# A macaron decoder block on one core: twelve up products of the second tile as three rounded passes, and the first seven-product tile with its low parts last

## The chip, the cores and the metric

The kernel runs on one core of one Trainium2 chip. TensorE (PE) multiplies 128x128 weight blocks with activations into PSUM; VectorE (DVE), ScalarE (ACT) and GpSimd (POOL) do the elementwise work; SP issues most of the loads from HBM, ACT and POOL a few. All transfers run on the core's 16 DMA engines; in the profile q1 is the queue that SP's issues use, q0 the one of POOL's. A transfer issued from POOL can add what it brings to what lies in SBUF already (an accumulating transfer). The metric is the device time of one execution in microseconds (us), lower is better.

## The reference, cut to what matters

```python
h = h + 0.5 * _swiglu(_rms_norm(h, ffn1_norm), ffn1_w_gate, ffn1_w_up, ffn1_w_down)
m, p, c, s = _hybrid_mixer(_rms_norm(h, mix_norm), ...)
h = h + m
h = h + 0.5 * _swiglu(_rms_norm(h, ffn2_norm), ffn2_w_gate, ffn2_w_up, ffn2_w_down)
y = _rms_norm(h, final_norm)
# _swiglu(x, wg, wu, wd) = (silu(x @ wg) * (x @ wu)) @ wd
```

520 tokens (512 of a prompt, 8 single ones), 1024 features, 2816 hidden features, all in float32. The change lies in the first feed-forward block, the first 45 us of the program.

## The kernel before, in words

Tokens are the columns of a product: two halves of 260. Features lie on the partitions, in eight groups of 128, which are also taken as four pairs: group j of the first depth half with group j of the second. A hidden tile is 128 hidden features; the block has 22 of them, named by f. Each needs a gate product and an up product over the 1024 features (u = 0 and 1); the weight of one is a 128x1024 float32 tile of 512 KB, `raw`, loaded by SP. There is room for two pairs of raws, so tile 2 takes the place of tile 0 and tile 3 that of tile 1, and each load waits until the readers of what lies there are done.

The opening handles tiles 0 and 1 with plain float32 products (`plain`): for each of gate and up there are 4 pairs x 2 depth halves x 2 token halves = 16 products of 128x260. On TensorE one plain product shows as two weight loads and two matmuls. The results are called P_00 (tile 0's gate), P_01 (its up), P_100 and P_101 (the two token halves of tile 1's gate) and P_11 (tile 1's up). P_11 comes last of the opening.

From tile 2 on the kernel splits each operand into a rounded part (hi) and the rest (lo) and multiplies hi by hi, hi by lo and lo by hi, in three passes of one record each (`mm3`, lines 147, 150 and 151). It also uses a scheme of seven products in place of eight over the 2x2 blocks of depth and tokens; the products are numbered 1 to 7 and run on tile 2 in the order 1, 2, 5, 6, 3, 7, then the first of tile 3, then 4. For it the weights are added up first: s1 (read as `c`) and s2 (read as `d`) are sums of quarters of the gate and up weights, so one tile needs the parts of four things: whi_a and wlo_a (the first raw), shi_c and slo_c, shi_d and slo_d, qhi_b and qlo_b (a quarter). Products 1 and 2 read a, 5 and 7 read c, 6 and 3 read d, 4 reads b.

The parts of a weight are made in one of two ways. `part` and `split` (line 135 and 137) cast hi on ScalarE and subtract on VectorE. `part_by_dma` (lines 242 to 244) casts hi on ScalarE, copies its negative into lo on ScalarE, and lets POOL add the weight from HBM to it by an accumulating transfer. For tile 2, s1 itself is made by transfers: SP brings two quarters and POOL adds a third (line 421).

The activations have been prepared in the same opening. Of each pair the four blocks of depth and token half lie in `xg`, slots 0 to 3; the rounded parts of slots 0, 1 and 2 (and of three sums, the rest of the seven) lie in xth (hi) and xtl (lo). Slot 3, the first depth half with the second token half, has no rounded part of its own.

A scheduler sets the order on each engine from the code, with priorities and a few fixed places (`tc.high_priority`, `queued`, `keep_in_program_order`); each engine then runs its own list in order, and an instruction that waits holds up all behind it on that engine. Around the change ScalarE runs the last casts of xth, a table load and two square roots for the norm (line 209), copies of P_00 to P_101, then the cast whi_2a, shi_2c, qhi_2b, another table load and the silu of tiles 0 and 1 (line 364). VectorE makes wlo_2a, the first half of s2 (line 425), slo_2c, the gate product of tile 0 (line 366), the second half of s2 (line 426), the gate product of tile 1 and slo_2d (both subtractions on line 137).

Of the kernel before, what the change touches and what calls it, by code (L numbers as in the profile page):

```python
# [10 lines left out]
F32 = mybir.dt.float32  # L11
F32R = mybir.dt.float32r
AF = mybir.ActivationFunctionType
ALU = mybir.AluOpType
# [3 lines left out]
P = 128  # L18
# [4 lines left out]
HB = NT // 2  # L23
HALVES = (slice(0, HB), slice(HB, NT))
KD = D // P
# [9 lines left out]
CHUNKS = (8, 8, 6)  # L35
LOW_ON_DVE = ((2, 0), (3, 0), (KF - 1, 1))
ON_ACT = 4
STATES = ((1, 1, 1, 1), (6, 17, 19, 20, 21), 4)
OUT_LOW_BY_DMA = ((1, 0), (1, 1))
LOW_BY_DMA = {1: (2, 3, 4, 5, 6), 2: (*range(7), 9, 11)}  # L40
# [24 lines left out]
def tile_trunk_step(ctx: ExitStack, tc: tile.TileContext, ins: dict, outs: dict):  # L65
    nc = tc.nc
# [9 lines left out]
    ps = [None]  # L76
# [43 lines left out]
    def weight_homes(n, name, hp, nb, tags):  # L120
        if hp is wp:
            popped = len(homes) > 1
            hp, nb, tags = homes.pop(0) if popped else homes[0]
            if third and not popped:
                third.append(name)
                if len(third) % 3 == 0:
                    return tuple(t[:, :n] for t in third[0])
        return tuple(hp.tile([P, 1024], F32R, tag=t, bufs=nb, name=f"{t}_{name}")[:, :n] for t in tags)

    def split(src, n, name, hp, nb, tags, then=()):  # L130
        hi, lo = weight_homes(n, name, hp, nb, tags)
        h, l = hi, lo
        if len(src.shape) == 3:
            h, l = (t.rearrange("p (j c) -> p j c", j=src.shape[1]) for t in (hi, lo))
        cast = nc.scalar.copy(h, src)  # L135
        with queued(*then):
            low = nc.vector.tensor_tensor(out=l, in0=src, in1=h.bitcast(F32), op=ALU.subtract)
        ends[:] = cast.ins, low.ins
        return hi, lo
# [23 lines left out]
    def ws(w, k, m=P):  # L163
        return w[:, k * m : (k + 1) * m]
# [76 lines left out]
    def part_by_dma(hi, lo, s, home):  # L241
        nc.scalar.copy(hi, s)
        nc.scalar.activation(out=lo, in_=hi.bitcast(F32), func=AF.Copy, scale=-1.0)
        nc.gpsimd.dma_start(out=lo, in_=home, accum_op=ALU.add)
# [22 lines left out]
    class Ffn:  # L267
# [26 lines left out]
        def plain(self, f, xg, j, us=(0, 1), pin=False):  # L294
            for u in us:
# [8 lines left out]
                for q in range(2):  # L304
                    for b, slot in enumerate(((0, 1), (3, 2))):
# [3 lines left out]
                        if pin and q == b == 0:  # L309
                            tc.keep_in_program_order(mm)  # L310

        def keep(self, f, us):

            for u in us:
                t = self.plain_kept[f, u] = self.gate_home(f) if u == 0 else self.wx.tile(
                    [P, 2, HB], F32, tag="ac", bufs=3, name=f"ac{self.i}_{f}")
                bs = self.banks[f, u]
                if len(bs) == 3:
                    copied = nc.scalar.copy(t, bs[2][:, :, :HB])
                else:  # L320
                    for b in range(2):
                        copied = nc.scalar.copy(t[:, b], bs[b][:, :HB])
            return copied.ins
# [77 lines left out]
        def sums(self, f, n, src, raw, d1, by_dma):  # L401
            i, wx = self.i, self.wx
            s1 = wx.tile([P, 2, 512], F32, tag="sw", bufs=3 - i, name=f"s1_{n}")
            s2 = wx.tile([P, 2, 512], F32, tag="sw", bufs=2, name=f"s2_{n}") if i == 1 else None
            if i == 2 and isinstance(f, int) and f < 4:
                s2 = self.qs[1].rearrange("p (q c) -> p q c", q=2)
            if isinstance(f, int):
                halves = [raw[:, u].rearrange("p (q c) -> p q c", q=2) for u in range(2)]
                up0 = halves[1][:, 0].unsqueeze(1).to_broadcast([P, 2, 512])
                diag = bass.AP(up0.tensor, up0.offset - 1024, [up0.ap[0], (1536, 2), up0.ap[2]])  # L410
            else:
                halves = [raw[:, u].rearrange("p (j q c) -> p q j c", q=2, c=P) for u in range(2)]
                up0 = halves[1][:, 0].unsqueeze(1).to_broadcast([P, 2, 4, P])
                diag = bass.AP(up0.tensor, up0.offset - 1024, [up0.ap[0], (1024 + P, 2), *up0.ap[2:]])
                s1, s2 = (t if t is None else t.rearrange("p q (j c) -> p q j c", j=4) for t in (s1, s2))
            if by_dma:
                low = src[2 * f + 1][:, :512].unsqueeze(1).to_broadcast([P, 2, 512])
                queue = nc.sync if i == 1 else nc.gpsimd
                queue.dma_start(out=s1[:, 0], in_=src[2 * f][:, :512])
                queue.dma_start(out=s1[:, 1], in_=src[2 * f + 1][:, 512:])  # L420
                nc.gpsimd.dma_start(out=s1, in_=low, accum_op=ALU.add)
            else:
                nc.vector.tensor_tensor(out=s1, in0=diag, in1=up0, op=ALU.add)  # L423
            s2 = halves[0] if s2 is None else s2
            nc.vector.tensor_tensor(out=s2[:, 0], in0=s1[:, 1], in1=halves[0][:, 0], op=ALU.add)
            nc.vector.tensor_tensor(out=s2[:, 1], in0=s2[:, 0], in1=halves[0][:, 1], op=ALU.add)
            flat = "p q c -> p (q c)" if isinstance(f, int) else "p q j c -> p (q j c)"
            s1 = s1.rearrange(flat)
            if len(s2.shape) == 3 or i == 1:
                s2 = s2.rearrange(flat)  # L430
            with tc.high_priority() if by_dma else nullcontext():
                e1 = split(s1, 1024, f"{n}c", wx, 2, ("shi", "slo"))
            e2 = split(s2, 1024, f"{n}d", wx, 2, ("shi", "slo"))
            if f == 2:
                self.behind[3] = tuple(ends), (), False
            first, second = (range(4), range(4, 8)) if isinstance(f, int) else (range(0, 8, 2), range(1, 8, 2))
            self.w[f] = {1: (d1, first), 2: (d1, second), 7: (e1, range(4)), 5: (e1, range(4, 8)), 6: (e2, range(4)),
                         3: (e2, range(4, 8))}
            self.held[f] = halves[1][:, 1]
            if i == 1:  # L440
                self.quarter(f)
# [17 lines left out]
        def product(self, f, p):  # L459
            js = range(KD // 2)  # L460
            if f not in self.A:
                self.load(f, *self.behind.get(f, ((), (), False)))
                n = f"{self.i}_{f}"
                self.A[f] = ps[0].tile([P, 512], F32, tag="A", bufs=2, name=f"A{n}")
                self.BE[f] = ps[0].tile([P, 2, 512], F32, tag="BE", bufs=2, name=f"BE{n}")
                self.ac[f] = [self.wx.tile([P, 2, HB], F32, tag="ac", bufs=3, name=f"ac{n}_{q}") for q in range(2)]
            if p != 1 and 4 not in self.w[f]:
                self.quarter(f)
            slot, dst, opens = {1: (0, 0, True), 2: (1, 1, True), 5: (3, 2, True), 6: (5, 0, False),
                                3: (2, 2, False), 7: (4, 0, False), 4: (6, 0, False)}[p]  # L470
            opens = opens and (p != 2 or f in self.whole)
            out = self.A[f] if dst == 0 else self.BE[f][:, dst - 1]
            (whi, wlo), k = self.w[f][p]
            xth, xtl = self.nx[:2]
            if isinstance(f, int):
                xs = [[x[:, j, slot] for j in js] for x in (xth, xtl)]
            else:
                u = {5: 6, 6: 5}.get(slot, slot)
                xs = [[self.gs[f.c * CHUNKS[0] // 2 + j][:, q, u] for j in js] for q in range(2)]
            wh, wl = ([ws(w, k[j]) for j in js] for w in (whi, wlo))  # L480
            pin = self.i == 1 or f != 1
            if self.i == 2:
                mm_low_last(out[:, :HB], wh, wl, *xs, opens, pin, skip_group_check=True)
            else:
                for j in js:
                    mm3(out[:, :HB], wh[j], wl[j], xs[0][j], xs[1][j], opens and j == 0, j == js[-1],
                        pin=pin and j == 0, skip_group_check=True)
            a, c = self.ac[f]
            if p == 1 and f not in self.whole:
                a = self.BE[f][:, :, :HB]  # L490
            keep = {1: a[:, 0], 6: a[:, 1], 7: c[:, 0], 5: c[:, 1]}.get(p)
            if keep is not None:
                self.copied = nc.scalar.copy(keep, out[:, :HB]).ins  # L493
                if (f, p) == (2, 7):
                    self.tail = self.copied
            if p == 7:
                nc.vector.tensor_tensor(out=c[:, 0], in0=c[:, 0], in1=c[:, 1], op=ALU.add)
# [226 lines left out]
    with tc.high_priority():  # L724
# [3 lines left out]
            late.pop(0)()  # L728
        with queued(root, recip):
            late.pop()()  # L730
    for j in range(KD // 2):
        ffn1.plain(1, xg1[j], j, (1,))
    with tc.high_priority(), queued(root):
        ffn1.keep(1, (0,))
    with tc.high_priority():
# [717 lines left out]
```

## Time and profile before

| what | value |
|---|---|
| median of 3 runs | 958.22 us (957.04 to 959.76) |
| the profiled execution | 956.44 us, span 954.7 us |
| granted TensorE clock in it | 0.996 |
| TensorE busy | 942.1 us, 7652 matmul records |
| VectorE / ScalarE busy | 854.0 us / 635.7 us |
| bytes read from HBM | 129.72 MB |

The span is the time between the first and the last instruction that the profiler saw. A row of instructions in order of time has its start, its length, the engine, the line, the operation and what it writes and reads; a bracket tells how long the engine sat idle before it and what ended that. Matmuls overlap, so their pace is read from start to start. A row of waits tells who waited for whom, the total in us, how often and the longest. A row of transfers ends with KB each and the median us from issue to landing; a row of a queue has packets, MB and the share of the 16 engines.

### The profile page before, as it was taken

The page shows a single profiled execution, that of the slowest core. Times are in us where ns is not written, and L with a number is a line of the kernel's source. Part 1 is how long each engine was busy: PE and PEld are TensorE (multiplying, and loading weights), DVE is VectorE, ACT ScalarE, POOL GpSimd, SP SyncE. Part 2 cuts the span into 40 slices and gives each one's busy share as a digit, 9 for nine tenths or more (in the row PEclk, how much of TensorE's full clock was granted, in tenths as well). Part 3 has the DMA queues.
Part 4 walks back from the last instruction along what each step waited for, and adds up shares of the span by engine and source line. Part 5 has one row for each costly group of instructions (what it writes and reads, how often), then busy time and mean ns, then how long its engine had stood idle before and what let it go on. Part 6 is the DMA issues. An engine that isn't in the chain of part 4 may idle for free. (4 is left out here: it accounts for less than half of the span.)

```text
span 954.7 us, 19636 instructions
## 1 busy us (share of the span) xinstructions
PE 942.1 (99%) x7652; PEld 925.0 (97%) x7652; DVE 854.0 (89%) x1462; ACT 635.7 (67%) x1178; POOL 148.9 (16%) x230
## 2 busy tenths in 40 slices
PE   9999999999999999999999999999999999999996
PEld 8999999999999999999999999999999999999995
DVE  6899899998988688789989998999989899899886
ACT  7777756677566465474768745777776766776763
POOL 0011100101000001046352000112122111122120
PEclk9999999999999999999999999999999999999998
DMA  7666554555553243353265444457667656767642
GB/s 213 179 164 154 141 157 125 122 137 151 141 147 101 81 139 116 90 185 133 97 179 163 119 121 122 112 122 179 170 165 183 158 124 158 183 166 188 171 147 90
DMA packets 53917, 138.34 MB, mean 145 GB/s; under 512 B 7672, under 2 KB 15800, under 8 KB 53824
## 3 DMA queue, kind: packets, MB, share of 16 engines
q1 hardware_dynamic: 39840, 104.18, 34.5%
q0 software_dynamic: 13712, 32.78, 18.5%
q8 instruction: 60, 0.98, 0.4%
q14 instruction: 33, 0.27, 0.1%
q10 hardware_dynamic: 272, 0.13, 0.0%
HBM read 129.72 MB, written 7.34 MB: 144 GB/s over the span
## 5 line engine op out<-in xcount | busy, mean ns | idle before, releaser
L493 ACT COPY ac<-A 128x260 f32<-128x260 f32 x85 | 31.7, 373 | 37.2 <-PE A L161 18.5
L423 DVE TENSOR_TENSOR s<-raw 128x1024 f32<-128x1024 f32 x39 | 47.5, 1218 | 2.7 <-DMA raw<-in_w1gu 1.4
L493 ACT COPY ac<-BE 128x260 f32<-128x260 f32 x41 | 15.4, 377 | 35.2 <-PE BE L161 16.9
L147 PE MATMUL inx<-xh_mx,whi_inx 128*128 128x260 f32 x112 | 31.8, 284 | 0.0
L150 PE MATMUL inx<-xl_mx,whi_inx 128*128 128x260 f32 x112 | 31.6, 282 | 0.0
L151 PE MATMUL inx<-xh_mx,wlo_inx 128*128 128x260 f32 x112 | 31.6, 282 | 0.0
L994 DVE SCALAR_TENSOR_TENSOR A<-U,h,A 128x544 f32<-128x544 f32 x36 | 28.9, 802 | 1.6 <-ACT A L992 1.2
L306 PE MATMUL P<-x,raw 128*128 128x260 f32 x128 | 28.9, 386 | 0.0
L306 PEld LDWEIGHTS P<-x,raw 128*128 128x128 f32 x128 | 24.5, 193 | 4.1 <-DMA raw<-in_w1gu 0.4
L1160 ACT ACTIVATE so<-br,sxdt 128x128 f32<-128x128 f32 x64 | 22.7, 376 | 7.7 <-DVE room L1162 6.9
L156 PE MATMUL wo<-catg,whi_wo 128*128 128x260 f32 x192 | 27.4, 285 | 0.0
L156 PEld LDWEIGHTS wo<-catg,whi_wo 128*128 128x128 f32 x192 | 24.8, 188 | 0.2
L135 ACT CAST thi<-raw 128x1024 fp32r<-128x1024 f32 (+1 forms) x14 | 14.2, 1013 | 15.3 <-PE wo L156 4.8
L1271 DVE TENSOR_TENSOR h<-wo,h 128x260 f32<-128x260 f32 x48 | 19.2, 422 | 5.0 <-PE wo L161 4.8
L248 DVE TENSOR_TENSOR gs<-gq,gs 128x780 fp32r<-128x780 f32 (+1 forms) x28 | 23.1, 826 | 0.0
L147 PE MATMUL inz<-xh_mx,whi_inz 128*128 128x260 f32 x80 | 22.9, 287 | 0.0
L150 PE MATMUL inz<-xl_mx,whi_inz 128*128 128x260 f32 x80 | 22.7, 284 | 0.0
L151 PE MATMUL inz<-xh_mx,wlo_inz 128*128 128x260 f32 x80 | 22.6, 283 | 0.0
L147 PEld LDWEIGHTS inx<-xh_mx,whi_inx 128*128 128x128 f32 x112 | 21.1, 188 | 0.2 <-issue 0.2
L156 PE MATMUL A<-xth_f,qs 128*128 128x260 f32 x84 | 21.2, 283 | 0.0
L156 PE MATMUL A<-xtl_f,qs 128*128 128x260 f32 x84 | 21.2, 284 | 0.0
L151 PEld LDWEIGHTS inx<-xh_mx,wlo_inx 128*128 128x128 f32 x112 | 21.1, 188 | 0.0
(3134 smaller groups left out, 4379.6 us busy)
## 6 DMA issues: line engine op xcount, KB each, us to landing
raw<-in_w2gu SPq DMA_DIRECT2D x44, 512.0 KB, 4.1
raw<-in_w1gu SPq DMA_DIRECT2D x41, 512.0 KB, 4.2
raw<-in_w_in SPq DMA_DIRECT2D x24, 512.0 KB, 3.5
raw<-in_w1d SPq DMA_DIRECT2D x16, 512.0 KB, 4.5
raw<-in_w2d SPq DMA_DIRECT2D x16, 512.0 KB, 4.6
raw<-in_w_out SPq DMA_DIRECT2D x12, 512.0 KB, 3.5
ab<-scr_acs SPq DMA_DIRECT2D x8, 512.0 KB, 4.9
h<-in_state_ssm SPq DMA_DIRECT2D x16, 256.0 KB, 3.5
```

What stands on the lines that cost most here:

```text
L135: cast = nc.scalar.copy(h, src)
L147: first = nc.tensor.matmul(ps, whi, xhi, start=start, stop=False, **kw)
L150: nc.tensor.matmul(ps, whi, xlo, start=False, stop=False, **kw)
L151: nc.tensor.matmul(ps, wlo, xhi, start=False, stop=stop, **kw)
L156: mm = nc.tensor.matmul(ps, w, x, start=start, stop=False, **kw)
L248: low = nc.vector.tensor_tensor(out=lo, in0=s, in1=hi.bitcast(F32), op=ALU.subtract)
L306: mm = nc.tensor.matmul(self.banks[f, u][b][:, :HB], ws(self.raw[f][:, u], j + 4 * q), xg[:, slot[q]], start=j == q == 0, stop=j == 3 and ...
L423: nc.vector.tensor_tensor(out=s1, in0=diag, in1=up0, op=ALU.add)
L493: self.copied = nc.scalar.copy(keep, out[:, :HB]).ins
L994: nc.vector.scalar_tensor_tensor(out=A[:, :n], in0=U[:, j : j + n], scalar=w(j), in1=A[:, :n], op0=ALU.mult, op1=ALU.add)
L1160: nc.scalar.activation(out=o[:, q], in_=br, func=AF.Copy, scale=sxdt[:, j, b : b + 1]))
L1271: nc.vector.tensor_tensor(out=h[:, d, hs], in0=ps[:, :HB], in1=h[:, d, hs], op=ALU.add)
```

## The change

Three things are changed, all in the first block.

Tile 1's up product P_11 is computed by the new `plain_split`. Its weight gets rounded parts whi_1p and wlo_1p, by `part_by_dma` (the constant `FIRST_BY_DMA` is true). The four products that read slot 3 stay plain and run first, on the raw. The twelve others are done in three passes each on the rounded parts, 36 records, in two groups: the first token half (16 passes with whi_1p, then 8 with wlo_1p), then the second depth half of the second token half (8, then 4).

Tile 2's products run by `mm_low_last` instead of `mm3`: of the twelve passes of a product the eight with the hi weight first, the four with the lo weight last.

And slo_2c gets an order: its subtraction is issued after the second half of s2.

```diff
+FIRST_BY_DMA = True
...
+        def plain_split(self, f, u, xg, by_dma):
+            src, raw = ins[f"w{self.i}gu"][2 * f + u], self.raw[f][:, u]
+            hi, lo = weight_homes(1024, f"{self.i}_{f}p", wp, 3, ("whi", "wlo"))
+            if by_dma:
+                part_by_dma(hi, lo, raw, src)
+            else:
+                part(hi, lo, raw)
+            t = ps[0].tile([P, 2, 512], F32, tag="BE", bufs=2, name=f"P{self.i}_{f}{u}")
+            self.banks[f, u] = [t[:, 0], t[:, 1], t]
+            js = range(KD // 2)
+            for j in js:
+                mm = nc.tensor.matmul(t[:, 1, :HB], ws(raw, j), xg[j][:, 3], start=j == 0, stop=False,
+                                      skip_group_check=True)
+            xs = [[x[:, j, k] for k in (0, 1) for j in js] for x in self.nx[:2]]
+            w = [[ws(p, k) for k in range(KD)] for p in (hi, lo)]
+            mm_low_last(t[:, 0, :HB], *w, *xs, True, skip_group_check=True)
+            xs = [[x[:, j, 2] for j in js] for x in self.nx[:2]]
+            mm_low_last(t[:, 1, :HB], *(p[KD // 2 :] for p in w), *xs, False, skip_group_check=True)
...
-            nc.vector.tensor_tensor(out=s2[:, 1], in0=s2[:, 0], in1=halves[0][:, 1], op=ALU.add)
+            total = nc.vector.tensor_tensor(out=s2[:, 1], in0=s2[:, 0], in1=halves[0][:, 1], op=ALU.add)
...
-                e1 = split(s1, 1024, f"{n}c", wx, 2, ("shi", "slo"))
+                e1 = split(s1, 1024, f"{n}c", wx, 2, ("shi", "slo"), (total.ins,) if by_dma and i == 1 else ())
...
-            if self.i == 2:
+            if self.i == 2 or f == 2:
                 mm_low_last(out[:, :HB], wh, wl, *xs, opens, pin, skip_group_check=True)
...
-    for j in range(KD // 2):
-        ffn1.plain(1, xg1[j], j, (1,))
+    ffn1.plain_split(1, 1, xg1, FIRST_BY_DMA)
```

Lines shift by up to 20 (line 209 becomes 210, 364 becomes 384, 425 becomes 445, 426 becomes 446). On POOL the accumulating transfer of wlo_1p stands between that of s and that of qlo_2b. SP's list is the same in number; the raw of tile 3 that takes the place of P_11's weight moves up by one place, since it now waits for the four plain products only. From tile 5 on the orders of the two programs are the same on all engines.

On ScalarE, before, from the last activation casts (xth) to the copies of the plain results:

```order
L230 ACTIVATE x_92<-h 128x520
L199 ACTIVATE sq<-h 128x520 x2
L247 CAST xth_f_87<-x_92 128x780 x2
L209 ACT_TABLE_LOAD
L209 ACTIVATE r_f_90<-psr_f_203,eps 128x260
L209 ACTIVATE r_f_90<-psr_f_207,eps 128x260
L319 COPY ac_0_236<-P_01_121 128x520
```

And in the changed kernel, the same stretch:

```order
L231 ACTIVATE x_92<-h 128x520
L200 ACTIVATE sq<-h 128x520 x2
L248 CAST xth_f_87<-x_92 128x780
L243 CAST whi_1p<-raw 128x1024
L248 CAST xth_f_87<-x_92 128x780
L244 ACTIVATE wlo_1p<-whi_1p 128x1024
L210 ACT_TABLE_LOAD
L210 ACTIVATE r_f_90<-psr_f_203,eps 128x260
L210 ACTIVATE r_f_90<-psr_f_207,eps 128x260
L339 COPY ac_0_236<-P_01_121 128x520
```

The cast and the negated copy of the new weight stand between and behind the last two casts of the activations, ahead of the table load.

On VectorE, before, from wlo_2a to the first sum of tile 3 (gq_0 is the gate of tiles 0 and 1, s_1_2_273 is s1 and s_1_2_274 is s2 of tile 2):

```order
L137 TENSOR_TENSOR wlo_2a<-raw,whi_2a 128x1024
L425 TENSOR_TENSOR s_1_2_274<-s_1_2_273,raw 128x512
L137 TENSOR_TENSOR slo_2c<-s_1_2_273,shi_2c 128x1024
L366 SCALAR_TENSOR_TENSOR gq_0_234<-ac_0_236,gq_0_234 128x2x260
L426 TENSOR_TENSOR s_1_2_274<-s_1_2_274,raw 128x512
L366 SCALAR_TENSOR_TENSOR gq_0_234<-P_11_242,gq_0_234 128x520
L137 TENSOR_TENSOR slo_2d<-s_1_2_274,shi_2d 128x1024
L423 TENSOR_TENSOR s_1_3_382<-raw 128x1024
```

And in the changed kernel:

```order
L138 TENSOR_TENSOR wlo_2a<-raw,whi_2a 128x1024
L445 TENSOR_TENSOR s_1_2_303<-s_1_2_302,raw 128x512
L386 SCALAR_TENSOR_TENSOR gq_0_234<-ac_0_236,gq_0_234 128x2x260
L446 TENSOR_TENSOR s_1_2_303<-s_1_2_303,raw 128x512
L138 TENSOR_TENSOR slo_2c<-s_1_2_302,shi_2c 128x1024
L386 SCALAR_TENSOR_TENSOR gq_0_234<-P_11_247,gq_0_234 128x520
L138 TENSOR_TENSOR slo_2d<-s_1_2_303,shi_2d 128x1024
L443 TENSOR_TENSOR s_1_3_411<-raw 128x1024
```

slo_2c has moved from ahead of the first gate product to behind the second half of s2.

## The prediction

> **What bounds the kernel now.** I read the page's head first, then the list of waits for TensorE's weight loads, then the opening engine by engine in order of time, and last the DMA queues. The head:
>
> ```profile
> span 954.7 us, 19636 instructions
> PE 942.1 (99%) x7652; PEld 925.0 (97%) x7652; DVE 854.0 (89%) x1462; ACT 635.7 (67%) x1178; POOL 148.9 (16%) x230
> ```
>
> TensorE is busy for 99% of the span, so time is won by giving it less work and lost by making it wait. What it waits for:
>
> ```profile
> PEld BE_Down(c=1, d=1)_10344 L156 <- ACT c_Down(c=1, d=1)_1_10346 L493: 1.5, 1, 1.5
> ...
> PEld P L306 <- DMA raw<-in_w1gu: 0.4, 1, 0.4
> ```
>
> In the opening there is one wait of 0.4 us. No later wait is long enough to swallow a shift of a microsecond that comes from the opening, and none of them starts from a fixed moment, so a shift of TensorE there should arrive at the end whole. The opening on TensorE, weight loads and matmuls:
>
> ```profile
> 23.35 10.49 PEld L306 LDWEIGHTS P<-x,raw 128*128 128x128 f32 x48
> ...
> 33.90 0.47 PE L147 MATMUL A<-xth_f,whi_2a 128*128 128x260 f32 x1
> 34.21 0.28 PE L150 MATMUL A<-xtl_f,whi_2a 128*128 128x260 f32 x1
> ...
> 36.97 0.28 PE L147 MATMUL BE<-xth_f,shi_2c 128*128 128x260 f32 x1
> ...
> 38.42 0.28 PE L147 MATMUL A<-xth_f,shi_2d 128*128 128x260 f32 x1
> ...
> 44.10 0.28 PE L151 MATMUL A<-xth_f,wlo_3a 128*128 128x260 f32 x1
> ```
>
> The last plain products stand without a gap against tile 2, whose first matmul starts at 33.90.
>
> **TensorE's work.** A plain product shows as two records: 48 in 10.49 us are 0.2186 us each, 0.437 us a product. Sixteen of them make up P_11, so it starts at 33.90 - 7.00 = 26.90. A pass on rounded parts costs 0.1206 us: from 34.21 to 44.10 there are 82 steps in 9.89 us. Twelve plain products go (-5.24 us), 36 passes come (+4.34): **-0.90 us**. The same 0.1206 a pass holds where low passes stand last, so the new order in tile 2 costs TensorE nothing by itself. With no wait, tile 2 starts at 33.00, and everything on TensorE behind it is 0.90 earlier.
>
> **The parts of the new weight.** ScalarE gets two passes over 128x1024: a cast like that of whi_2a below (1.05 us) and a negated copy. For the copy the nearest rows are that cast, 1.05, and the 128x512 copy of qlo_2b, 0.62; I take 1.0.
>
> ```profile
> 18.30 1.57 ACT L247 CAST xth_f<-x 128x780 fp32r<-128x780 f32 x2
> 19.89 1.28 ACT L209 ACT_TABLE_LOAD   x1
> 23.34 0.92 ACT L209 ACTIVATE r_f<-psr_f,eps 128x260 f32<-128x260 f32 x2 [2.17 <-PE psr_f L206]
> ...
> 30.05 1.05 ACT L135 CAST whi_2a<-raw 128x1024 fp32r<-128x1024 f32 x1 [2.35 <-DMA raw<-in_w1gu]
> ...
> 33.88 0.64 ACT L364 ACTIVATE gq<-gq 128x520 f32<-128x520 f32 x1
> 34.42 0.62 ACT L243 ACTIVATE qlo_2b<-qhi_2b 128x512 fp32r<-128x512 f32 x1
> ...
> 35.88 1.05 ACT L135 CAST shi_2d<-s 128x1024 fp32r<-128x1024 f32 x1 [0.32 <-DVE s L426]
> ```
>
> Both stand ahead of the table load at 19.89, behind which ScalarE idled for 2.17 us until the sums of squares came. The 2.0 us fit there with 0.2 to spare: nothing on ScalarE is later at 23.34. If 0.3 us more were needed, the next idle stretch, 2.35 us ahead of whi_2a, would take it. The copy ends at about 21.9, and POOL can issue the accumulating transfer then; it issued that of s from 20.05 to 21.41, so it is free.
>
> ```profile
> 20.05 1.36 POOL L421 DMA_DIRECT2D s<-in_w1gu  x1 [19.59 <-DMA s<-in_w1gu]
> ...
> 22.89 0.33 SPq L384 DMA_DIRECT2D raw<-in_w1gu  x1
> ...
> 25.52 0.33 SPq L384 DMA_DIRECT2D raw<-in_w1gu  x1
> ```
>
> The high passes of P_11 run after the four plain products, so its first low pass comes at 26.90 + 4 x 0.437 + 16 x 0.1206 = 30.58. That is when wlo_1p has to lie in SBUF.
>
> **The transfer and what stands behind it.** This is the term that decides. The queues from 20 to 25 us, the later raw of tile 2 from its own stretch, and then the nearest case, an accumulating transfer of the same 512 KB with two raws issued behind it, from 97 to 102 us and in two stretches:
>
> ```profile
> q0 software_dynamic: 237, 0.49, 60.6%
> issues: line engine op xcount, KB each, median us to landing
> s<-in_w1gu POOLq DMA_DIRECT2D x1, 512.0 KB, 6.1
> raw<-in_w1gu SPq DMA_DIRECT2D x1, 512.0 KB, 4.9
> ```
>
> ```profile
> raw<-in_w1gu SPq DMA_DIRECT2D x1, 512.0 KB, 4.5
> ```
>
> ```profile
> q0 software_dynamic: 139, 0.52, 66.0%
> q1 hardware_dynamic: 19, 0.08, 4.0%
> issues: line engine op xcount, KB each, median us to landing
> raw<-in_w1d SPq DMA_DIRECT2D x2, 512.0 KB, 5.8
> wlo_Down(c=0, d=0)a<-in_w1d POOLq DMA_DIRECT2D x1, 512.0 KB, 5.5
> ```
>
> ```profile
> 98.50:102.00 3.50, 3.50 (x32) 3.50 (x31) 2.90 (x7) 2.94 (x6) 0.00 (x0) 1.00 1.00 172
> 102.00:104.50 2.50, 2.50 (x23) 2.50 (x23) 2.50 (x6) 2.42 (x5) 0.00 (x0) 1.00 0.97 393
> ```
>
> The last three numbers of a stretch are the clock, the DMA engines' share and GB/s. Up to 25 us all bytes are q0's, POOL's queue, though SP had issued a raw at 22.89; up to 102 us q1, SP's queue, has 0.08 MB against 0.52. So raws wait until an accumulating transfer is nearly through; then two of them move in 2.5 us. The accumulation itself keeps the engines full for 3.5 us.
>
> wlo_1p is issued at 21.9, behind s in the same queue; s lands at 20.05 + 6.1 = 26.15, wlo_1p 3.5 us later, at 29.65. That is 0.9 ahead of 30.58: no wait there. But the raws of tile 2 now stand behind 512 KB more. The one issued at 25.52 is what whi_2a waits for: before, it landed at 25.52 + 4.5 = 30.02. In the nearest case the first raw took 5.8, 1.3 more than 4.5: that is one estimate of its delay X. The other: it is the second raw behind the accumulation. There the first landed 1.3 us after the accumulation (98.02 + 5.8 against 97.01 + 5.5) and the second has half of 2.5 us more to move: 29.65 + 1.3 + 1.25 = 32.2, X = 2.2. I take the middle, **X = 1.8**. The ends are 0 (the transfer fits in between) and 2.2, and 4.2 in the slower rival below.
>
> **What X does.** whi_2a is in front of ScalarE's queue; behind it stand shi_2c, qhi_2b, a table load and the silu at 33.88, for which VectorE waits:
>
> ```profile
> 31.13 1.23 DVE L137 TENSOR_TENSOR wlo_2a<-raw,whi_2a 128x1024 fp32r<-128x1024 f32 x1 [0.41 <-ACT whi_2a L135]
> ...
> 32.87 1.22 DVE L137 TENSOR_TENSOR slo_2c<-s,shi_2c 128x1024 fp32r<-128x1024 f32 x1
> 34.55 0.70 DVE L366 SCALAR_TENSOR_TENSOR gq<-ac,gq 128x520 f32<-128x520 f32 x1 [0.46 <-ACT gq L364]
> 35.17 0.68 DVE L426 TENSOR_TENSOR s<-s,raw 128x512 f32<-128x512 f32 x1
> 35.77 0.69 DVE L366 SCALAR_TENSOR_TENSOR gq<-P,gq 128x520 f32<-128x520 f32 x1
> 36.97 1.22 DVE L137 TENSOR_TENSOR slo_2d<-s,shi_2d 128x1024 fp32r<-128x1024 f32 x1 [0.51 <-ACT shi_2d L135]
> ```
>
> All of this comes X later. Moreover slo_2c now stands behind L426 instead of in the idle time ahead of 34.55: it starts at 35.77 + X and ends at 36.99 + X, and after the second gate product slo_2d runs from 37.5 + X to 38.7 + X (1.14 and 0.61 us from start to start, as at 31.13 and 34.55). TensorE needs shi_2d at 38.42 - 0.90 = 37.52, where 35.88 + 1.05 + X meets it up to X = 0.6; slo_2c after eight high passes, at 36.97 - 0.90 + 0.96 = 37.03; slo_2d at 37.52 + 0.96 = 38.48. The largest lateness counts, since a wait moves the later needs along: 38.7 + X - 38.48 = 0.25 + X. Low parts last buys these 0.96 us; one by one the low part would be wanted at 0.24.
>
> **Sum.** -0.90 + 0.25 + X = X - 0.65; with X = 1.8, **+1.15 us**. Tile 3's second raw is issued earlier than before, since P_11 lets go of its buffer after the plain products; it lands behind the raws above and was off the path, so I count nothing. The profiled execution took 956.44 us, its span 954.7 and 1.74 around it; it would be 957.6. The median of the runs shown is 958.22, 1.78 above it: **959.4**.
>
> **The rivals.**
>
> *The queues share.* If q1 takes turns with q0, the raws move beside wlo_1p. From 25 us on 3.5 us of accumulation and the two raws run at half rate each, the raws through 5.0 us: data by 30.1. The first raw of the nearest case had half of its stretch, 1.25 us, behind it at 103.25 and landed at 98.02 + 5.8 = 103.82, 0.6 later; so 30.7 here, X = 0.7: +0.05, 958.3. Against it stand q1's 0.08 MB beside 0.52; for it, that q1 isn't shut out at the end of that stretch. The Trainium skill, "DMA: Bandwidth & Descriptors", section "Queues, rings and completion order", says that each DMA engine goes round robin between the queue rows that have work, packet by packet. By that rule this rival would be the forecast; the rows of 20 to 25 and 97 to 102 us show no such turns.
>
> *All covered.* X below 0.3: +0.25 - 0.90 = -0.65, or the whole -0.90 if VectorE is 0.25 faster than I count: 957.3 to 957.6. For it speaks that s and the first raw are done early; against it that the engines have no 3.5 us free ahead of 30.02.
>
> *Slower.* The accumulation is as slow as the slowest of its kind:
>
> ```profile
> DMA to landing us min/median/max: 3.6/4.9/7.9
> ```
>
> 7.9 instead of 5.5 is 2.4 more on everything behind it: X = 4.2, +3.55, 961.8. It decides as slower from X = 3.5, a landing of the raw at 33.5. wlo_1p at 32.05 would itself stop TensorE for 1.5 us, inside that sum. Against it: that kind of case stands in other stages, and s took 6.1 here.
>
> **How the numbers follow.** Raws behind the accumulation 0.50 (959.4); sharing 0.17 (958.3); covered 0.13 (957.3 to 957.6); slower 0.14 (961.8); 0.06 for a gain beyond what I find, from 2.9 us on, which nothing in the opening has to give. About 0.3%, 2.9 us, is what a measurement can tell from no change: the runs shown lie from 957.04 to 959.76. The first three are within it: 0.80. The range leaves out the last two: 957.2 to 961.4, from the whole gain of 0.90 to X = 2.2 with as much as the runs differ.
>
> **What would show it.** P_11 from 26.9 with 4 plain products and 36 passes, without a gap ahead of its low ones; wlo_1p landing by 30.6; whi_2a starting near 31.9 instead of 30.05; TensorE waiting for slo_2c or slo_2d, some 2 us in all, with what follows about 1.2 later than now, the row at 44.10 at 45.2 to 45.3. A whi_2a at 30.0 and no wait in tile 2 would make it wrong to the fast side, a wait ahead of wlo_1p to the slow side.

## The result and the profile after

The changed kernel took 960.82 us (median of 14 executions, 956.24 to 962.28) against 957.07 us of the kernel before (14 executions, 955.13 to 960.16). The ratio is 1.0023, 95% interval 1.0013 to 1.0034: some 2.2 us more. The interval leaves out 1, so the loss is real, but it is below the 0.3% that the prediction takes as the line to no change, and 960.82 is inside the predicted range. The executions of the changed kernel fall into two groups, 956.2 to 958.0 (6) and 960.7 to 962.3 (8), so its median alone tells less than the ratio, which compares the means; the lower group's mean is 0.2 us below that of the kernel before, the upper group's 3.9 above it. The profiled execution, at 960.71 us, is of the upper group.

Head of the page after:

```profile
span 958.9 us, 19663 instructions
PE 943.2 (98%) x7664; PEld 925.7 (97%) x7664; DVE 853.9 (89%) x1462; ACT 637.5 (66%) x1180; POOL 149.4 (16%) x231
```

The span is 4.2 us longer. Where tile 3 begins a loss of this size is there already; before, it began here:

```profile
42.78 0.28 PE L147 MATMUL A<-xth_f,whi_3a 128*128 128x260 f32 x1
```

After, it begins 4.48 us later, at 47.26. The weight loads of the opening that had to wait:

```profile
32.49 1.02 PEld L162 LDWEIGHTS P<-xth_f,wlo_1p 128*128 128x128 f32 x8 [1.94 <-DMA wlo_1p<-in_w1gu]
40.15 0.54 PEld L162 LDWEIGHTS BE<-xth_f,slo_2c 128*128 128x128 f32 x4 [1.38 <-DVE slo_2c L138]
41.31 0.19 PEld L157 LDWEIGHTS A<-xth_f,shi_2d 128*128 128x128 f32 x1 [0.63 <-ACT ac L513]
```

The matmuls of the four plain products, and the first ones of tiles 2 and 3:

```profile
26.95 1.92 PE L324 MATMUL P<-x,raw 128*128 128x260 f32 x8
...
34.99 0.28 PE L157 MATMUL A<-xth_f,whi_2a 128*128 128x260 f32 x1
...
47.26 0.28 PE L148 MATMUL A<-xth_f,whi_3a 128*128 128x260 f32 x1
```

In these three places TensorE waits where before it did not: for wlo_1p, for slo_2c, and for `ac`, ScalarE's copy of a result of product 1, which must be out of its PSUM bank before product 6 may write there. ScalarE's rows from the new passes on, and its copy `ac`:

```profile
20.63 1.05 ACT L244 ACTIVATE wlo_1p<-whi_1p 128x1024 fp32r<-128x1024 f32 x1
21.70 1.28 ACT L210 ACT_TABLE_LOAD   x1
23.20 0.92 ACT L210 ACTIVATE r_f<-psr_f,eps 128x260 f32<-128x260 f32 x2 [0.22 <-PE psr_f L207]
...
33.16 1.05 ACT L136 CAST whi_2a<-raw 128x1024 fp32r<-128x1024 f32 x1 [5.59 <-DMA raw<-in_w1gu]
...
39.95 1.04 ACT L136 CAST whi_3a<-raw 128x1024 fp32r<-128x1024 f32 x1
40.90 0.37 ACT L513 COPY ac<-A 128x260 f32<-128x260 f32 x1
```

VectorE's rows of the two low parts, 3.11 us behind slo_2c's forecast without a delay (35.77) and as late behind slo_2d's (37.5):

```profile
38.88 1.22 DVE L138 TENSOR_TENSOR slo_2c<-s,shi_2c 128x1024 fp32r<-128x1024 f32 x1
...
40.62 1.22 DVE L138 TENSOR_TENSOR slo_2d<-s,shi_2d 128x1024 fp32r<-128x1024 f32 x1
```

And the same copy before, with the cast that it is queued behind:

```profile
36.84 1.05 ACT L135 CAST whi_3a<-raw 128x1024 fp32r<-128x1024 f32 x1
37.79 0.37 ACT L493 COPY ac<-A 128x260 f32<-128x260 f32 x1
```

whi_2a starts 3.11 us late (33.16 against 30.05), and the copy `ac` exactly as late (40.90 against 37.79): from the landing of tile 2's raw to this copy ScalarE's list is one chain, with one stop of 0.32 us for VectorE's second half of s2, which hangs on the same chain and is the same in both. TensorE goes on 0.41 us after the copy's start, at 41.31. Before, that would have been 37.79 + 0.41 = 38.20, and TensorE wanted the bank at 38.42, so the copy had 0.22 us to spare. Product 6 then starts 41.31 - 38.42 = 2.89 us late, which is 3.11 - 0.22. From its start to tile 3 it took 5.95 us, before 4.36: 1.59 more. The clock there (length of the stretch, busy time and instructions of PE, PEld, DVE, ACT and POOL, then the granted clock, DMA share and GB/s):

```profile
42.00:45.40 3.40, 3.40 (x18) 3.40 (x17) 3.37 (x4) 0.38 (x1) 0.00 (x0) 0.51 0.53 150
```

For 3.4 us TensorE ran at half its clock: 18 matmuls lie in the stretch, against 30 in the second profile of the same kernel, shown below. So the 4.48 us are 2.89 of ScalarE's chain and 1.59 of the clock.

The loss does not stay at 4.48 us. Tile 4 starts 4.24 us late and tile 6 4.98, since TensorE waits once more in between, for the low part of tile 4's quarter, which POOL makes by an accumulating transfer of 256 KB. The kernel before does not wait there:

```profile
69.74 0.19 PEld L152 LDWEIGHTS A<-xth_f,qlo_4b 128*128 128x128 f32 x1 [0.68 <-DMA qlo_4b<-in_w1gu]
```

Tile 20 is 4.94 late, and some 0.7 us come back behind it; where was not followed.

The transfers that made whi_2a late. POOL's two, in the stretch from 20.5 to 22.5 us (KB, and us from issue to landing):

```profile
s<-in_w1gu POOLq DMA_DIRECT2D x1, 512.0 KB, 6.7
wlo_1p<-in_w1gu POOLq DMA_DIRECT2D x1, 512.0 KB, 10.5
```

SP's issue of the raw that whi_2a reads:

```profile
25.39 0.33 SPq L404 DMA_DIRECT2D raw<-in_w1gu  x1
```

The queues from 24 to 26 us, and the landing of that raw (a queue's share adds up the times of its packets, so it can pass 100%):

```profile
q0 software_dynamic: 160, 0.33, 111.1%
issues: line engine op xcount, KB each, median us to landing
raw<-in_w1gu SPq DMA_DIRECT2D x1, 512.0 KB, 7.8
```

q0 moved alone there, though SP had issued a raw at 22.76 too. In the same stretch before, q1 moved more than q0:

```profile
q0 software_dynamic: 129, 0.23, 64.1%
q1 hardware_dynamic: 83, 0.34, 44.2%
```

After that the queues share. The changed kernel from 26 to 28 us:

```profile
q1 hardware_dynamic: 93, 0.37, 57.4%
q0 software_dynamic: 46, 0.07, 20.7%
```

And from 28 to 30 us:

```profile
q0 software_dynamic: 76, 0.31, 79.4%
q1 hardware_dynamic: 61, 0.20, 27.1%
```

So the raw of whi_2a landed at 25.39 + 7.8 = 33.2 instead of 30.0, and wlo_1p at 32.5.

### The profile page after: what moved, and what is told of

Read it like the earlier page. It is cut to its first block, busy times and chain, and to the rows that moved or that the text cites. A ratio compares the mean times of both kernels' runs of the same rounds, so it can differ in the third digit from the quotient of the medians.

```text
span 958.9 us, 19663 instructions
## 1 busy us (share of the span) xinstructions
PE 943.2 (98%) x7664; PEld 925.7 (97%) x7664; DVE 853.9 (89%) x1462; ACT 637.5 (66%) x1180; POOL 149.4 (16%) x231
## 5 line engine op out<-in xcount | busy, mean ns | idle before, releaser
L307 PE MATMUL P<-x,raw 128*128 128x260 f32 x96 | 21.6, 384 | 0.2 <-DMA raw<-in_w1gu 0.2
L522 DVE TENSOR_TENSOR BE<-BE,ac 128x260 f32<-128x260 f32 (+1 forms) x41 | 18.4, 449 | 3.7 <-PE BE L162 2.0
L307 PEld LDWEIGHTS P<-x,raw 128*128 128x128 f32 x96 | 18.1, 190 | 3.3 <-DMA raw<-in_w1gu 0.6
```

The costliest lines, as they stand in the source:

```text
L307: mm = nc.tensor.matmul(self.banks[f, u][b][:, :HB], ws(self.raw[f][:, u], j + 4 * q), xg[:, slot[q]], start=j == q == 0, stop=j == 3 and ...
```

## The experiments

**The theories.** A: the accumulating transfer of wlo_1p is the cause; it holds up the raws of tile 2, and everything on ScalarE behind them. B: the order is, slo_2c's place behind the second half of s2. C: the half clock that follows the waits makes a part of it. Each run below lists, beside its ratio, where whi_2a and `ac` start and where tile 3 does (30.05, 37.79 and 42.78 before).

**The changed kernel once more**, against other executions of the kernel before.

> The changed kernel itself once more, on the chip of these runs. Theory A: whi_2a starts 1.5 us or more after 30.0 and TensorE waits in tile 2. Theory C: where its profile shows waits of some 2 us within 3.4 us, the clock is 0.5 for 3.4 us after them; where the waits are shorter, it stays at 1.00, and tile 3 starts earlier than at 47.3 by 1.7 us or more. Ratio 1.001 to 1.003.

Ratio 1.0020 (1.0009 to 1.0031); 959.28 against 956.48 us. Its two longest waits in tile 2 (a third, for wlo_2a, is 0.22 us):

```profile
39.01 0.54 PEld L162 LDWEIGHTS BE<-xth_f,slo_2c 128*128 128x128 f32 x4 [1.71 <-DVE slo_2c L138]
40.17 0.19 PEld L157 LDWEIGHTS A<-xth_f,shi_2d 128*128 128x128 f32 x1 [0.62 <-ACT ac L513]
```

ScalarE:

```profile
32.01 1.05 ACT L136 CAST whi_2a<-raw 128x1024 fp32r<-128x1024 f32 x1 [4.55 <-DMA raw<-in_w1gu]
...
39.75 0.37 ACT L513 COPY ac<-A 128x260 f32<-128x260 f32 x1
```

And the stretch that ran at half clock in the other profile:

```profile
42.00:45.40 3.40, 3.40 (x30) 3.40 (x30) 3.37 (x5) 2.36 (x4) 0.00 (x0) 1.00 0.20 52
```

Here wlo_1p landed 8.7 us after its issue at 21.84, at 30.54, and TensorE did not wait for it; whi_2a and `ac` are both 1.96 late, product 6 starts 1.75 late, the clock stays at 1.00, and tile 3 is 1.80 late, at 44.58. So the wait for wlo_1p, the size of the delay and the half clock differ between executions of one kernel; the chain from whi_2a to `ac` is there in both.

**No accumulating transfer**: the low part of wlo_1p is made by VectorE.

```diff
-FIRST_BY_DMA = True
+FIRST_BY_DMA = False
```

> wlo_1p made by a subtraction on VectorE, no transfer; everything else as in the changed kernel. Theory A (the accumulating transfer delays itself and the raws of tile 2): no wait ahead of the low passes of P_11, whi_2a back from 33.2 to 30.0 us, TensorE's clock at 1.00 through tile 2, a wait of at most 0.5 us for slo_2d, and about 0.5 us less than the kernel before (ratio 0.9995). Theory B (the cost is slo_2c's later place on VectorE): the wait for slo_2c stays at over 1 us and the time is above that of the kernel before by 1 us or more.

Ratio 0.9996 (0.9981 to 1.0010). whi_2a at 30.11, tile 3 at 42.70 (15.1 us from P_11's first matmul at 27.63, 15.7 from 27.08 before; this execution's opening began 0.55 us later). In tile 2 one wait is left, not at slo_2d, where I had expected it:

```profile
38.27 0.19 PEld L157 LDWEIGHTS A<-xth_f,shi_2d 128*128 128x128 f32 x1 [0.34 <-ACT ac L513]
```

The loss is gone with the transfer. But the gain of 0.90 us on TensorE did not come in either: the copy `ac`, at 37.85, lets product 6 begin 0.15 earlier than before and no more. Tiles 4 and 5 start 0.30 early, then the wait for qlo_4b stands in this run too (0.72 us), and tile 6 starts 0.50 late.

**The transfer alone**: the kernel before, with the two passes of ScalarE and the transfer issued and their results not read.

```diff
+    unread = weight_homes(1024, "1_1p", wp, 3, ("whi", "wlo"))
+    part_by_dma(*unread, ffn1.raw[1][:, 1], ins["w1gu"][3])
     for j in range(KD // 2):
         ffn1.plain(1, xg1[j], j, (1,))
```

> The kernel before, with P_11 plain and tile 2 as it was, plus only the parts of P_11's weight, whi_1p and wlo_1p, which nothing reads. Theory A: whi_2a starts at about 33 us instead of 30.0, TensorE waits for wlo_2a at tile 2's start (1.0 to 1.5 us) and for slo_2d (together about 2.6 us), and the time is 2.6 us above that of the kernel before, 1.7 more if the clock halves for 3.4 us. Theory B: no change, within 0.3 us.

Ratio 1.0021 (1.0010 to 1.0032), as much as the whole change. Its one wait in the tile:

```profile
39.95 0.19 PEld L147 LDWEIGHTS A<-xth_f,shi_2d 128*128 128x128 f32 x1 [1.01 <-ACT ac L493]
```

Its ScalarE:

```profile
31.79 1.04 ACT L135 CAST whi_2a<-raw 128x1024 fp32r<-128x1024 f32 x1 [3.52 <-DMA raw<-in_w1gu]
...
39.53 0.37 ACT L493 COPY ac<-A 128x260 f32<-128x260 f32 x1
```

whi_2a and `ac` are 1.74 late, tile 3 1.61 (44.39). I had expected whi_2a later, near 33, and waits at wlo_2a and slo_2d; the one wait stands at `ac`. Theory A holds. The negated copy on ScalarE comes and goes with the transfer in these two runs, but ScalarE idled 3.52 us ahead of whi_2a here, so the copy is not what made it late. Whether the accumulating matters or only the 512 KB was not tried with a plain transfer. The run shows more: TensorE still has the 0.90 us of work here and loses about as much as with it saved, since `ac` sets the time in both.

**Half the transfer**: the low part's second half by POOL (256 KB), its first by VectorE.

```diff
-                part_by_dma(hi, lo, raw, src)
+                n = 512
+                nc.scalar.copy(hi, raw)
+                nc.scalar.activation(out=lo[:, n:], in_=hi[:, n:].bitcast(F32), func=AF.Copy, scale=-1.0)
+                nc.gpsimd.dma_start(out=lo[:, n:], in_=src[:, n:], accum_op=ALU.add)
+                nc.vector.tensor_tensor(out=lo[:, :n], in0=raw[:, :n], in1=hi[:, :n].bitcast(F32), op=ALU.subtract)
```

> The changed kernel with half of the low part by an accumulating transfer (256 KB), half on VectorE. Theory A, cost by bytes: whi_2a starts about half as late, near 31.3 us (30.0 without a transfer, 31.6 to 33.3 with 512 KB), wlo_1p lands before its low passes want it, and the time lies between: ratio 1.000 to 1.001. Rival (an accumulating transfer costs a turn in the queues, whatever its size): whi_2a as late as with 512 KB, ratio 1.002.

Ratio 1.0005 (0.9994 to 1.0015). whi_2a at 30.58 (0.53 late), `ac` at 38.32 (0.53), tile 3 at 43.15 (0.37): between none and all of it, below the half that I expected of the delay. TensorE did not wait for wlo_1p, as expected.

**slo_2c early again**: its place ahead of the first gate product, as before the change.

```diff
-                e1 = split(s1, 1024, f"{n}c", wx, 2, ("shi", "slo"), (total.ins,) if by_dma and i == 1 else ())
+                e1 = split(s1, 1024, f"{n}c", wx, 2, ("shi", "slo"))
```

> The changed kernel without slo_2c's tie to the second half of s2: slo_2c is made again in the idle time before the gate product. Theory B: the wait for slo_2c goes and with it 1.2 us or more of time. Theory A: the wait moves to slo_2d, which still hangs on the raw that lands late; time within 0.5 us of the changed kernel.

Ratio 1.0016 (1.0001 to 1.0030). The wait for slo_2c is gone, and two others stand in its place:

```profile
PEld A L157 <- ACT shi_2d L136: 1.2, 1, 1.2
PEld A L162 <- DVE slo_2d L138: 0.8, 1, 0.8
```

whi_2a is 1.55 late, tile 3 1.01. Theory B looks like no main cause: with the place undone most of the loss remains, by a ratio whose interval is too wide to tell how much. The order on ScalarE changes with it too: the copy `ac` now stands ahead of shi_2d (37.02), and tile 3 is no longer tied to it.

**Low parts last alone**: the kernel before with `mm_low_last` in tile 2 and P_11 plain.

```diff
-            if self.i == 2:
+            if self.i == 2 or f == 2:
                 mm_low_last(out[:, :HB], wh, wl, *xs, opens, pin, skip_group_check=True)
```

> The kernel before with one part of the change alone: tile 2's products with the low passes last. All theories: no pass is added or dropped and nothing was waited for, so tile 3's first matmul (its row with whi_3a) stays at 42.8 us and the ratio at 1.000. If the order of passes has a price of its own on TensorE, tile 3 starts later without a wait in the rows.

Ratio 1.0005 (0.9995 to 1.0014), tile 3 at 42.85. By itself that part does nothing that can be measured. TensorE waits 0.2 us for `ac`, which I had not expected: whi_2a starts 0.22 late although no transfer was added, so X varies by that much without one.

**TensorE kept busy in the wait for slo_2c**: the changed kernel with six products of ones, which nothing reads, ahead of the four passes that read slo_2c.

```diff
+        for _ in range(fill):
+            tc.keep_in_program_order(nc.tensor.matmul(idle[0][:, :P], ones, ones, start=True, stop=True))
```

> The changed kernel with six 128x128 products of ones by ones, read by nothing, ahead of the low passes of tile 2's product 5, where TensorE waited 1.4 us for slo_2c: they keep it busy for 1.3 us. Theory C (the waits in tile 2 halve TensorE's clock): the granted clock stays at 1.00 from 41 to 46 us, the waits' ends stay where they are, and the time falls by up to 1.7 us against the changed kernel (half of 3.4 us). Rival (the clock falls for a reason of its own, or only profiled executions show it): clock 0.5 for 3.4 us as before, and time the same or longer.

Ratio 1.0013 (0.9997 to 1.0029). This execution is the twin of the profiled one of the changed kernel: wlo_1p waited for as long, whi_2a even later. Its waits:

```profile
32.70 1.02 PEld L166 LDWEIGHTS P<-xth_f,wlo_1p 128*128 128x128 f32 x8 [1.81 <-DMA wlo_1p<-in_w1gu]
...
41.50 0.19 PEld L159 LDWEIGHTS A<-xth_f,shi_2d 128*128 128x128 f32 x1 [0.63 <-ACT ac L522]
```

Its clock in the stretch in question:

```profile
42.00:45.40 3.40, 3.40 (x31) 3.40 (x30) 3.37 (x5) 1.43 (x2) 0.00 (x0) 1.00 0.62 175
```

Product 6 starts later than there, 41.50 against 41.31, and yet tile 3 starts earlier, 45.91 against 47.26: 4.41 us from the one to the other instead of 5.95. The clock stayed at 1.00. That is theory C's price. That the waits made the clock fall, and that filling one of them kept it up, is not shown by this. In the profiled execution the clock falls at 42.06 us, is back at 45.47 and falls again at 953.42, behind the last matmul: 3.41 and 907.95 us apart, 1 and 266 steps of 3.413. The step ahead of the first fall holds both waits. Counted back in such steps from the fall at the end of the second profile (949.65), the step with most of its waits is the second row:

```profile
38.64:42.06 3.42, 1.84 (x13) 1.42 (x13) 3.42 (x5) 2.58 (x5) 0.66 (x1) 1.00 0.62 90
38.28:41.70 3.42, 2.27 (x16) 2.07 (x17) 3.42 (x4) 2.11 (x4) 0.00 (x0) 1.00 0.86 165
```

So waits of like length, lying otherwise to the steps, left 1.84 us of matmuls in the one and 2.27 in the other, and only behind the first did the clock fall. In the run with the idle products (fall at the end at 954.96) a step ends at 40.19, between its two waits, so that even unfilled they would have lain in different steps. And its step from 29.95 to 33.36, with the wait for wlo_1p, has 1.80 us of matmuls and is followed by the full clock. How little work makes the clock fall stays open, and with it whether the idle products did anything.

The mean clock of an execution is 0.996 to 0.998 for the kernel before (88 executions whose clock is known) and for the other variants (94, this run's 12 among them), and below that in 8 of the 26 of the changed kernel. A stretch of 3.4 us at half clock is worth 0.0018 of it, about what 0.996 and 0.998 differ by, so others of the 26 can have had one. By the eight alone it would be 0.5 us on the mean (an estimate: 8/26 of 1.59), of 1.9 to 2.2.

**Towards a better version**: no accumulating transfer and slo_2c early, and then slo_2d also ahead of tile 3's first sum on VectorE.

```diff
-FIRST_BY_DMA = True
+FIRST_BY_DMA = False
...
-                e1 = split(s1, 1024, f"{n}c", wx, 2, ("shi", "slo"), (total.ins,) if by_dma and i == 1 else ())
+                e1 = split(s1, 1024, f"{n}c", wx, 2, ("shi", "slo"))
```

> The changed kernel without the accumulating transfer (low part on VectorE) and without slo_2c's tie. Theory A: the 0.9 us of TensorE's work come out whole: from the start of P_11 to tile 3's first matmul 15.0 us, where the kernel before has 15.9 and the version with the tie 15.3; ratio about 0.9990, hardly to be told from 1. Rival (the three passes cost more than their pace tells, or another wait turns up in tile 2): 15.9 or more.

```diff
-                self.behind[3] = tuple(ends), (), False
+                self.behind[3] = tuple(ends), tuple(ends[1:]) if i == 1 else (), False
```

> The changed kernel with the low half of the first up chunk subtracted by VectorE (no accumulating transfer), slo_2c's subtraction early, and slo_2d's subtraction placed on VectorE ahead of tile 3's first sum of partial results. In the run with the first two of these edits TensorE still waited 0.47 us for slo_2d and 0.52 of the 0.90 us were gained. Theory that the 0.90 us less of TensorE's work is all there and only that last wait keeps part of it: no wait of more than 0.1 us in tiles 1 and 2, from the start of the root-mean-square sum's weight loads to tile 3's first matmul 19.4 us (20.30 before, 19.78 with the wait), ratio to the kernel before 0.9985 to 0.9995. Rival: the low halves of tile 3, which stand later on VectorE by this edit, are late in its turn; then TensorE waits 0.3 to 0.6 us in tile 3 or 4 and the ratio stays at 0.9995 to 1.0005.

The first: 0.9996 (0.9983 to 1.0009), tile 3 at 42.06. The second: 0.9994 (0.9984 to 1.0004), tile 3 at 41.40. In both, `ac` is out of the way, as ScalarE's rows of the first show:

```profile
35.30 0.36 ACT L513 COPY ac<-A 128x260 f32<-128x260 f32 x1
35.72 1.05 ACT L136 CAST shi_2d<-s 128x1024 fp32r<-128x1024 f32 x1
```

The whole openings of these executions began up to 0.34 us earlier than before, so I count from the weight loads of the sum of squares, which stand 4.60 to 4.61 us ahead of P_11's first matmul in every run with the new P_11 (here at 22.28 and 22.14). Before they stood here, so P_11 began at 27.08:

```profile
22.48 0.85 PEld L206 LDWEIGHTS psr_f<-acc_f,ones 128*128 128x128 f32 x4
```

To tile 3 it took 20.30 before, 19.78 in the first, where TensorE still waited 0.47 for slo_2d, and 19.26 in the second, 1.04 less than before. From P_11's first matmul (26.88 and 26.74) it is 15.18 and 14.66, against 15.70 before (not 15.9, as the first expectation has it). But in the second the rival came in too, with a wait in tile 3, and behind it the wait for qlo_4b:

```profile
46.73 0.19 PEld L152 LDWEIGHTS A<-xth_f,slo_3d 128*128 128x128 f32 x1 [0.78 <-DVE slo_3d L138]
...
64.75 0.19 PEld L152 LDWEIGHTS A<-xth_f,qlo_4b 128*128 128x128 f32 x1 [0.69 <-DMA qlo_4b<-in_w1gu]
```

The work saved is real, and these two waits take it back: from the span's start, tile 3 begins 1.38 us earlier than in the kernel before, tile 4 0.75 earlier and tile 6 0.07 later. The first version has no wait for qlo_4b in its profile; there tile 6 is 0.96 earlier and the span 1.0 shorter (953.7). That wait is in six of the ten profiles of other kernels than the one before, those in which the transfer of qlo_4b took 7.4 to 7.8 us from issue to landing; in the others, the kernel before among them, it took 6.5 to 7.0. What makes it slower was not tried. By their ratios neither version can be told from the kernel before.

**The runs together.** X is how much later than 30.05 whi_2a starts. In the runs where `ac` stands behind whi_3a on ScalarE, tile 3 should come X - 0.22 later:

| run | X | `ac` late by | X - 0.22 | tile 3 late by |
|---|---|---|---|---|
| changed kernel, profiled | 3.11 | 3.11 | 2.89 | 4.48 (1.59 of it the clock) |
| changed kernel once more | 1.96 | 1.96 | 1.74 | 1.80 |
| TensorE kept busy | 3.29 | 3.29 | 3.07 | 3.13 |
| transfer alone | 1.74 | 1.74 | 1.52 | 1.61 |
| half the transfer | 0.53 | 0.53 | 0.31 | 0.37 |
| low parts last alone | 0.22 | 0.22 | 0.00 | 0.07 |
| no accumulating transfer | 0.06 | 0.06 | -0.16 | -0.08 |

Seven runs with and without the saved 0.90 us, with and without the wait for wlo_1p, agree within 0.1 us. So up to tile 3 neither of these two decides anything in them.

## Why the prediction came out as it did

The forecast class, about the same and on the slow side, was right, and so was the cause: raws delayed by the accumulating transfer. 1.0023 and 1.0020 are 2.2 and 1.9 us; forecast was +1.15.

- **The number.** That 960.82 lies in the range is in part luck. The forecast stood on 958.22, the median of three executions; fourteen gave 957.07. By the medians the change is +3.75, more than the +3.2 at which the range ends above 958.22. And the mean of +2.2 is made of a group at -0.2 and one at +3.9; +1.15 is neither.
- **TensorE's work, -0.90.** Right as work, and a little too small. P_11 began at 27.08 before and not at 26.90: 48 weight loads in 10.49 us are 47 steps of 0.219 and one load of 0.19, and the first matmul of tile 2 starts close behind the last plain one. The 26.95 of the changed kernel meets the forecast because its opening began 0.14 earlier. The first low pass is wanted at 32.49 - 1.94 = 30.55 (30.58 forecast). The run without any wait in tiles 1 and 2 got 1.04 less, since in it the passes of tile 2 are 0.1196 us apart (72 in the 8.61 us from 32.79 to 41.40) and not 0.1206. What the sum took from it is another matter, as the lateness below shows.
- **ScalarE's two passes fit.** Right, to the tenth: the negated copy took 1.05, and 0.22 us of idle time are left ahead of the square root (0.2 forecast).
- **wlo_1p at 29.65.** Too early: 30.54 once and 32.5 once. The step that failed is that the transfer follows s by 3.5 us with the engines to itself. s landed at 20.85 + 6.7 = 27.55 in the profiled execution, and wlo_1p 4.95 after it, since the raws moved beside it from 26 us on. The wait that this made, 1.94 us, was named as what would make the forecast wrong to the slow side; by the table it cost nothing, as ScalarE's chain ended later still.
- **X = 1.8.** 1.96 in one profile, 3.11 in another, beyond the end of 2.2. That the transfer delays the raws is right, as the runs with and without it show. That the raws wait until it is nearly through is not: q1 moved 0.37 MB beside 0.07 from 26 to 28 us, long before wlo_1p landed at 32.5. So that 1.8 is near 1.96 is luck in part. The rival of sharing queues had X at 0.7 and doesn't give these delays, though its premise is half right: q1 moved nothing from 24 to 26 us and took its turns from then on. The Trainium skill, "DMA: Bandwidth & Descriptors", section "Queues, rings and completion order", has each DMA engine go round robin between the queue rows that have work; the rows from 26 to 30 us agree with it, those of 24 to 26 us don't show it. Sharing only moved the delay about: wlo_1p later, the raws no earlier.
- **The largest lateness, slo_2d's 0.25 + X.** This is the step of the sum that failed. The latest in tile 2 is the copy `ac`: behind shi_2d and whi_3a on ScalarE it lets product 6 start at 38.20 + X, where the sum needed 37.52, so its lateness is 0.68 + X. I followed the weights' parts alone and did not ask what product 6 writes over. Put right, the sum is X - 0.22 in place of X - 0.65: with my X +1.58, with that of the second profile +1.74, where 1.80 was measured.
- **Not foreseen at all:** the half clock, 1.59 us in the profiled execution.
- **The shift at the end.** That the shift arrives at the end whole holds only roughly: tile 3 is 4.48 and 1.80 late, the spans are 4.2 and 2.1 longer, but between them lies the wait for qlo_4b (0.68 and 0.3 us), which the forecast does not have.

What stays open is why wlo_1p and the raws land two microseconds later in some executions (10.5 and 10.4 us for wlo_1p in two profiles, 8.7 in three). In the late ones POOL issued the transfer of s at 20.85 and 21.11 instead of 20.18 to 20.57, as the transfer that it waits for had landed later; what delayed that was not tried, nor whether it makes the two groups of times. The clock alone does not make them: the upper group has mean clocks of 0.994 to 0.998, the lower one of 0.996 and 0.997.

## What to carry to other kernels

Before crediting an engine with saved work, look for the chain that stands just behind it: here ScalarE's list, a chain from a landing raw to a copy out of PSUM, had only 0.22 us to spare, so of 0.90 us saved on TensorE no more could count while that copy stood where it did. With the copy out of the way the next chains came up, first a low part in VectorE's list and then a transfer. When asking what a product waits for, list what it writes over as well as what it reads. And a transfer added beside a busy stretch is paid by the next load in line, so its price is read at the consumer of that load, not at its own.

## What the runs showed of the hardware

In one execution TensorE ran at half its clock for 3.41 us behind two waits of 1.38 and 0.63 us, some 0.5 us apart. In the second profile of the same kernel 1.71 and 0.62 us were not followed by it. The changes of the clock in the first trace lie whole steps of 3.413 us apart (42.06, 45.47 and 953.42). The Trainium skill, "TensorE: Matmul & The Clock Gate", Part 1, says that a free-running window of about 3.4 us decides, and that the clock falls to half after an idle window. The steps and the length of the slow stretch agree, and a free-running window would explain that like waits do it in one execution and not in the next; but the step ahead of the fall was far from idle, with matmuls in 1.84 of its 3.42 us, and a step with 1.80 us in another run passed at the full clock. Where the line lies no run here shows.

An accumulating transfer of 512 KB took 8.7 to 10.5 us from issue to landing behind another of its kind, and from 24 to 26 us, with the engines full, its queue moved 0.33 MB, while the plain raws moved 0.84 MB in the 2 us from 32 to 34:

```profile
q1 hardware_dynamic: 235, 0.84, 103.2%
```
